# A two-layer attention trunk on one core: a second projection by seven block products, its root in a diagonal matrix, and three smaller moves

## The chip, the core and the metric

The kernel runs on one core of a Trainium2 chip. The metric is the device time of one execution in microseconds. A core has TensorE (PE, with its weight loads PEld), VectorE (DVE), ScalarE (ACT), GpSimd (POOL) and SyncE (SP), and 16 DMA engines that move data between HBM and the on-chip memories SBUF and PSUM. [...]

## The reference

256 tokens of width 2048 go through two layers and a final norm. Cut to what matters:

```python
h = x
h = h + gla_mixer(rms_norm(h, gla_norm), ...)        # layer 0
h = h + retention_mixer(rms_norm(h, ret_norm), ...)  # layer 1
return rms_norm(h, final_norm)

def gla_mixer(h, w_in, w_a1, w_a2, b_a, head_g, w_out):
    q, k, v, gate = split(h @ w_in)                  # 1024, 1024, 4096, 4096 columns
    log_a = log_sigmoid((h @ w_a1) @ w_a2 + b_a) / 16   # low-rank gate, rank 16
    o = chunked gated linear attention(q, k, v, log_a)  # 4 heads of 256 keys and 1024 values
    o = o * rsqrt(mean(o * o, -1) + EPS)             # per head and token
    return (o * head_g * silu(gate)) @ w_out         # 4096 -> 2048
```

The retention layer has the same outline: 8 heads of 256 keys and 512 values, rotary q and k, a group norm and a gated output projection of 4096 to 2048.

## The kernel before

**Precision.** Weights come from HBM as fp32 tiles `raw` of 2 x 128 x 512 elements (512 KB). `emit_split` turns each into a high part `hi` (ACT, L298) and a low part `lo` (DVE, L299). Activations lie in SBUF as such pairs too, transposed: `xhl` for layer inputs and `ogt` for gated head outputs, each with 16 tiles (kt) of 128 contraction rows x 256 tokens. Every product of a weight tile and an activation tile is three matmuls (high x high, high x low, low x high): L341 to L343 in plain groups, L412 to L414 in block products. Plain fp32 products appear only in small places, such as the scores' `pair_mm` (L763) and the transposes (L707) by an identity matrix.

**Plain and seven-product columns.** A plain group of 512 columns (`group_x`) runs eight weight tiles, 12 matmuls each. `out_pair` and `values_and_gates` treat two column groups together: the contraction's first half (kt 0 to 7) is a 2 x 2 block product, tokens by columns, made of seven block products (P1, P2, P3, P5, P6, P7, P8, of two weight tiles and 12 matmuls each) instead of eight; the second half runs directly (`direct`: v4 to v7 and g4 to g7, 12 matmuls for one weight tile). P1, P2 and P8 use the activations as they are; P3, P5, P6 and P7 use sums and differences of token blocks, which `make_sums` prepares (DVE and ACT) and splits. On the weights' side the sums are made in the raw tiles, by accumulating DMAs of POOL's queue and by DVE (L293). The order of the weight tiles is written out in strings such as `UNIT = "P1 v4 z P3 v5 P5 v6 P6 P2 v7 P7 g4 g5 P8 g6 g7"`; `_plan` turns the whole kernel's order into a list of loads and buffers beforehand. `next_weights` keeps the splits `LOOK = 3` tiles ahead, in four buffers for `hi` and `lo` each.

**Side work.** Latency-bound pieces are generators in `side` (GLA) or `tasks` (retention); `advance` runs one step of the first at set places between weight tiles, `drain_side` all that is left. A scheduler then sets each engine's order from this program order, the data's readiness in its own model and marks such as `high_priority`; `keep` holds instructions in program order, and `first` puts instructions at the front.

**Order.** Layer 0 runs heads 0 and 1, then the first half of its output projection (`out_half` "ga"), heads 2 and 3, and the second half ("gb"). Layer 1 does the same with four heads each, and ends with `out_last` and `out_tail`. `JOINT` says which value/gate groups and which column pairs go by seven products: in "gb" columns 0 and 1 are plain, 2 and 3 a pair.

**Head outputs.** `gla_head` makes each head's outputs in two groups of 512 columns: `o_part` (attention output, sums of squares `sso`), then `og_part`: the root `hr` of the head's mean square, `o * hr * silu(gate)` (L895), and `transpose_out` into `ogt`, four transposes for each half, with the head's scale applied on the way out (ACT L500, DVE L501). For head 3 this happens while "gb" is already running on kt 0 to 7.

**Low-rank gate.** `first_group` runs beside the first q/k group. At j = 0 it splits `w_a1` into `wa1` (ACT L613, DVE L614), and from j = 1 on it issues two `zps` products (L640) for each step, for the x tiles that `make_xhl` (L546, L549) has made.

**The tail.** The last 512 output columns are done last (`out_tail`), one half of the tokens t after the other. `tail_banks` puts the residual into PSUM first: one bank for t = 0, two banks of 256 columns for t = 1, whose matmuls are all 256 wide. Then come squares of both halves (ACT L1163), the product with the final norm's weights (DVE L1164), the root (`rsqrt_col`, L1125 to L1130), and the scaling of all columns (L1178, L1180) with their DMAs out.

Of the kernel before, what the change touches and what calls it, by code (L numbers as in the profile page):

```python
# [64 lines left out]
def _plan():  # L65
# [41 lines left out]
    def out_cols_of(name, half, cut, joint):  # L107
        for c in (0, 2):
            cols = [(name, half, c + n) for n in range(2)]
            if joint[c // 2]:  # L110
                pair(cols[1], cols[0])
# [45 lines left out]
UNIT = "P1 v4 z P3 v5 P5 v6 P6 P2 v7 P7 g4 g5 P8 g6 g7"  # L157
MIXED = "q0 q1 P1 q2 q3 q4 z P5 q5 P6 q6 q7 P2 P3 v4 v5 v6 P7 v7 g4 g5 P8 g6 g7"
WHOLE = " ".join(f"q{j}" for j in range(NSUB)) + " " + UNIT


def ret_order(h):
# [8 lines left out]
    ("ao", 0): (True, True),  # L171
    ("ao", 1): (False, True),
    ("ro", 0): (False, True),
# [5 lines left out]
def kernel(  # L179
# [260 lines left out]

    def make_sums(lhs, name, where):
        s = cur["s"] = [None] * 4
        room = where(name)
# [164 lines left out]
    def first_group(j):  # L608
        if j == 0:
            for kt in (2, 3):  # L610
                make_xhl(kt)
            first(
                nc.scalar.activation(wa1[:, :, 0:16], wa1_src, AF.Copy),  # L613
                nc.vector.tensor_tensor(  # L614
                    wa1[:, :, 32:48], wa1_src, wa1[:, :, 0:16].bitcast(F32), ALU.subtract
                ),
            )
        if j == 3:
# [4 lines left out]
        if j == 6:  # L623
# [7 lines left out]
            for hh in range(2):  # L631
# [5 lines left out]
                wa2.append(t)  # L637
        kts = range(2 * (j - 1), 2 * j) if j < NSUB - 1 else range(2 * (j - 1), NKT)
        for kt in kts if j else ():
            mm(zps, wa1[:, kt, :], xhl[:, kt, :, :], start=kt == 0, stop=kt == NKT - 1)  # L640
# [59 lines left out]

    def transpose_out(src, kt0, scale0, dst, name):
        for half in range(2):
            tp = mis_p.tile([P, 2, SEQ], F32, tag="mis", name=f"{name}_tp{half}")
            for jj in range(2):
                j = half * 2 + jj
                for t in range(2):
                    nc.tensor.transpose(  # L707
                        tp[:, jj, t * P : (t + 1) * P], src(t, j), ident
                    )
            kt = kt0 + half * 2  # L710
# [125 lines left out]
    def gla_head(h):  # L836
# [43 lines left out]
        def og_part(gj):  # L880
            g = 2 * h + gj
            if gj == 0:
# [9 lines left out]
            o, sg, hr = os_[gj], sgs[gj], hw["hr"]  # L892
            with tc.high_priority():
                for t in range(2):
                    nc.vector.scalar_tensor_tensor(  # L895
                        o[:, t, :], o[:, t, :], hr[:, t : t + 1], sg[:, t, :], ALU.mult, ALU.mult
                    )
            yield
# [4 lines left out]
                ogt,  # L903
                f"got{g}",
            )
# [72 lines left out]
    def tail_banks(t):  # L978
        w = GW // 2 if t else GW
        ps = acc(2, f"tail_ps{t}", (P, w), which=[2, 3]) if t else acc(1, f"tail_ps{t}", which=[1])  # L980
        for n, p in enumerate(ps):
            keep(nc.scalar.activation(p, cur["resid"][:, t, 3 * GW + n * w : 3 * GW + (n + 1) * w], AF.Copy))
        return ps

    def out_pair(c, first, name, final=False):
        lhs, s = ogt, cur["s"]
# [37 lines left out]
        product(A, plain(0, 0), stop=True)  # L1024
        advance()
        direct(lhs, (C, V1), 4)
        join(g, 0, A)
        advance()
        product(C, summed(0))
        advance()  # L1030
        direct(lhs, (C, V1), 5)
        drain_side()
        product(P5, summed(1), stop=True)
        direct(lhs, (C, V1), 6)
        for t in range(2):
            join(c, t, P5)
        product(A, summed(2), stop=True)
        product(B, plain(4, 0))
        join(c, 0, A, ALU.subtract)
        direct(lhs, (C, V1), 7, stop=True)  # L1040
        product(A, summed(3), stop=True)
# [25 lines left out]
        if onward:  # L1067
            for _ in late[0]:
                pass
            tasks.append(out_transposes(g))  # L1070
        begun.clear()
# [26 lines left out]
    def out_half(first, final, name, cut=0, hook=None, joint=(False, False)):  # L1098
        pend = {}
        for c in range(4):  # L1100
            if joint[c // 2]:
                if c % 2 == 0:
                    out_pair(c, first, name)
                continue
# [27 lines left out]
    def out_tail():  # L1132
# [5 lines left out]
        for t in range(2):  # L1138
# [4 lines left out]
            for j in range(HEAD, NSUB):  # L1143
                if t == 0:
                    kept.append(next_weights())
                hi, lo = kept[j - HEAD]
                if t == 0:
                    for q in range(SUB):
                        mm3(ps[0], ogt, j * SUB + q, t, hi, lo, q, HEAD * SUB)
                    continue  # L1150
                cols = [slice(0, half), slice(half, GW)]
                order = [(q, n) for q in range(SUB) for n in range(2)]
                if j == NSUB - 1:
                    order = [(q, n) for n in range(2) for q in range(SUB)]
                for q, n in order:
                    mm3(ps[n], ogt, j * SUB + q, t, hi[:, :, cols[n]], lo[:, :, cols[n]], q, HEAD * SUB)
            sq = st_p.tile([P, 2], F32, tag="sq", name=f"sq{t}")
            last = o_p.tile([P, 2, GW], F32, tag="o", name=f"last{t}")[:, 0, :]
            for n in range(2):
                at = slice(n * half, (n + 1) * half)  # L1160
                src = ps[n] if t else ps[0][:, at]
                junk = sg_p.tile([P, half], F32, tag="sg", name="sqj")
                nc.scalar.activation(junk, src, AF.Square, accum_out=sq[:, n : n + 1])  # L1163
                nc.vector.tensor_tensor(last[:, at], src, fns[3][:, at], ALU.mult)  # L1164
                if n == 0:
                    nc.vector.tensor_scalar(pre[:, 2:3], sq[:, 0:1], 1.0 / D, pre[:, 1:2], ALU.mult, ALU.add)
            rf = fin[:, 0, t : t + 1]
            rsqrt_col(rf, sq[:, 1:2], pre[:, 2:3], f"nf{t}")
            for piece, src, which in (
# [6 lines left out]
                src = cur["resid"][:, t, piece] if src is None else src  # L1176
                if which == "v":
                    nc.vector.tensor_scalar(src, src, rf, None, ALU.mult)  # L1178
# [281 lines left out]
    for h in range(2, 4):  # L1460
        gla_head(h)
    get_resid("gb_resid")
    slots = deque((2, 3, 0, 1))
    out_half(False, False, "gb", joint=JOINT["ao", 1])
# [123 lines left out]
```

## Time and profile before

| | |
|---|---|
| median of 3 runs | 1374.34 us (1373.69 to 1375.95) |
| profiled execution | 1373.26 us, span of the profile 1371.5 us |
| granted TensorE clock | 0.999 |
| PE busy | 1362.3 us, 99% |
| PEld, DVE, ACT, POOL busy | 1145.0, 1098.4, 847.0, 136.8 us |
| moved by DMA | 315.04 MB, mean 230 GB/s |

A row of a timeline has the start and duration in us, engine, line, operation, output<-inputs, shape and count, and in brackets the idle time of the engine before it with what ended it. A row of the groups has count, busy time, mean ns of one, and idle time before. A row of a stretch has, for each engine, busy us and instructions. L12 is line 12 of the kernel before.

### The profile page before, as it was taken

What the parts mean: (1) busy time and instruction counts of PE and PEld (TensorE: products, weight loads), DVE (VectorE), ACT (ScalarE), POOL (GpSimd) and SP (SyncE); (2) the same over time, 40 slices, a digit from 0 to 9 for tenths busy, and PEclk for the clock granted to TensorE, in tenths of its full rate; (3) what the DMA queues carried; (4) which work ended last, traced back from release to release, by engine and by line L of the source; (5) the groups of instructions that cost most, each with busy time, mean ns of one, the idle gap of its engine ahead of it and who ended that gap; (6) DMA issues with size and microseconds to landing.
All of it is one profiled execution on the core that took longest, in us unless ns stands there. A gap on an engine that the chain in (4) does not pass through costs nothing.

```text
span 1371.5 us, 18372 instructions
## 1 busy us (share of the span) xinstructions
PE 1362.3 (99%) x6564; PEld 1145.0 (83%) x6564; DVE 1098.4 (80%) x1520; ACT 847.0 (62%) x1119; POOL 136.8 (10%) x194
## 2 busy tenths in 40 slices
PE   9999999999999999999999999999999999999997
PEld 8888888888888888888888888888888888888886
DVE  6686795987878896769887988897867897889796
ACT  6576656656567756656666576655546665666565
POOL 1003020110021021001011010100101101010010
PEclk9999999999999999999999999999999999999999
DMA  9755566789658667868897878796798797979773
GB/s 358 259 175 168 169 208 184 156 247 318 200 153 262 204 204 183 319 169 232 267 331 197 260 202 249 207 316 218 172 367 219 240 261 197 259 198 317 241 176 124
DMA packets 84508, 315.04 MB, mean 230 GB/s; under 512 B 9776, under 2 KB 10800, under 8 KB 83136
## 3 DMA queue, kind: packets, MB, share of 16 engines
q1 hardware_dynamic: 67200, 241.63, 50.4%
q0 software_dynamic: 15920, 64.89, 23.9%
q10 hardware_dynamic: 1296, 7.35, 1.4%
q8 instruction: 51, 0.84, 0.2%
q14 instruction: 41, 0.34, 0.1%
HBM read 303.35 MB, written 10.49 MB: 229 GB/s over the span
## 4 chain that ended last, share of the span: by engine, by line
PE 99%; DMA 1%; DVE 0%; ACT 0%; DVEq 0%; issue 0%; ACTq 0%
PE rqk_ps L384 8%; PE re_ps L412 8%; PE re_ps L413 8%; PE re_ps L414 8%; PE rqk_ps L385 4%; PE gqk_ps L384 4%; PE gg_ps L342 3%; PE gv_ps L343 3%; PE gv_ps L341 3%; PE gv_ps L342 3%; PE gg_ps L341 3%; PE gg_ps L343 3%; PE ge_ps L412 2%; PE ge_ps L413 2%; PE ge_ps L414 2%; PE gae_ps L413 2%
## 5 line engine op out<-in xcount | busy, mean ns | idle before, releaser
L299 DVE TENSOR_TENSOR lo<-raw,hi 128x1024 fp32r<-128x1024 f32 (+1 forms) x568 | 687.4, 1221 | 215.5 <-ACT hi L298 205.5
L298 ACT ACTIVATE hi<-raw 128x1024 fp32r<-128x1024 f32 (+1 forms) x568 | 595.9, 1055 | 394.3 <-DMA raw<-in_w_all 50.8
L384 PE MATMUL rqk_ps<-xhl,hi 128*128 128x512 f32 x480 | 162.9, 397 | 0.0
L413 PE MATMUL re_ps<-lo,xhl 128*128 128x512 f32 x352 | 137.5, 391 | 0.0
L414 PE MATMUL re_ps<-hi,xhl 128*128 128x512 f32 x352 | 137.3, 390 | 0.0
L310 POOL DMA_DIRECT2D raw<-in_w_all x90 | 78.0, 868 | 556.1 <-DVE lo L299 222.1
L412 PE MATMUL re_ps<-hi,xhl 128*128 128x512 f32 x352 | 132.6, 391 | 0.0
L385 PE MATMUL rqk_ps<-xhl,lo 128*128 128x256 f32 x480 | 122.5, 281 | 0.0
L384 PEld LDWEIGHTS rqk_ps<-xhl,hi 128*128 128x128 f32 x480 | 89.7, 188 | 17.8
L385 PEld LDWEIGHTS rqk_ps<-xhl,lo 128*128 128x128 f32 x480 | 87.6, 189 | 3.4
L414 PEld LDWEIGHTS re_ps<-hi,xhl 128*128 128x128 f32 x352 | 66.1, 188 | 13.6
L413 PEld LDWEIGHTS re_ps<-lo,xhl 128*128 128x128 f32 x352 | 66.2, 188 | 13.2
L412 PEld LDWEIGHTS re_ps<-hi,xhl 128*128 128x128 f32 x352 | 66.0, 188 | 13.2
L384 PE MATMUL gqk_ps<-xhl,hi 128*128 128x512 f32 x216 | 76.6, 399 | 0.0
L342 PE MATMUL gg_ps<-lo,xhl 128*128 128x512 f32 x192 | 75.5, 393 | 0.0
L342 PE MATMUL gv_ps<-lo,xhl 128*128 128x512 f32 x192 | 75.3, 392 | 0.0
L341 PE MATMUL gv_ps<-hi,xhl 128*128 128x512 f32 x192 | 75.2, 393 | 0.0
L343 PE MATMUL gv_ps<-hi,xhl 128*128 128x512 f32 x192 | 75.1, 391 | 0.0
L343 PE MATMUL gg_ps<-hi,xhl 128*128 128x512 f32 x192 | 75.0, 391 | 0.0
L341 PE MATMUL gg_ps<-hi,xhl 128*128 128x512 f32 x192 | 74.9, 392 | 0.0
L829 POOL TENSOR_TENSOR s<-s,m 128x64 f32<-128x64 f32 x56 | 36.1, 676 | 232.5 <-DVE m L820 223.2
L385 PE MATMUL gqk_ps<-xhl,lo 128*128 128x256 f32 x216 | 59.1, 281 | 0.0
(434 smaller groups left out, 2659.8 us busy)
## 6 DMA issues: line engine op xcount, KB each, us to landing
raw<-in_w_all SPq DMA_DIRECT2D x449, 512.0 KB, 4.9
raw<-in_w_all POOLq DMA_DIRECT2D x90, 512.0 KB, 6.8
resid<-in_x_n SPq DMA_DIRECT2D x2, 1024.0 KB, 10.8
gg<-in_gn_g POOLq DMA_DIRECT2D x8, 256.0 KB, 4.2
resid_x<-resid ACTq DMA_DIRECT2D x1, 2048.0 KB, 7.9
gb<-in_gn_b POOLq DMA_DIRECT2D x8, 256.0 KB, 6.0
gb_resid<-resid_x POOLq DMA_DIRECT2D x1, 2048.0 KB, 11.3
resid_g<-gb_resid ACTq DMA_DIRECT2D x1, 2048.0 KB, 10.5
```

What stands on the lines that cost most here:

```text
L298: a = nc.scalar.activation(hi[:, sl], src[:, sl], AF.Copy)
L299: b = nc.vector.tensor_tensor(lo[:, sl], src[:, sl], hi[:, sl].bitcast(F32), ALU.subtract)
L310: nc.gpsimd.dma_start(raws[n], block(key), accum_op=ALU.add)
L341: pin(mm(ps, xh, hi[:, q, :], start=kt == 0, stop=False, **onto))
L342: pin(mm(ps, xh, lo[:, q, :], start=False, stop=False, **onto))
L343: pin(mm(ps, xl, hi[:, q, :], start=False, stop=kt == end - 1, **onto))
L384: mm(ps[c], wh, rhs[:, kt, :, :], start=kt == 0, stop=False)
L385: mm(ps[c][:, 0, :], wl, rhs[:, kt, 0, :], start=False, stop=False)
L412: pin(mm(ps, xh, hi[:, q, :], start=start, stop=False, **again))
L413: pin(mm(ps, xh, lo[:, q, :], start=False, stop=False, **again))
L414: pin(mm(ps, xl, hi[:, q, :], start=False, stop=stop, **again))
L829: nc.gpsimd.tensor_tensor(dst, dst, side_of(m[:, li, :], z), ALU.add)
```

## The change

It has five parts. (1) Columns 0 and 1 of "gb" become a pair by seven products, in a new order `LATE` that has P1, P2, P3 first and the tiles kt 8 to 15 (v4 to v7) late. Its sums ("osum2") are made in five steps within the last value/gate stage of head 3 (group 7) and serve columns 2 and 3 too. (2) For head 3, `o` is multiplied by the gate without the root; the root goes into a diagonal matrix that takes the identity's place, so the transposes become fp32 matmuls. (3) `wa1` is split at j = 2, and the `zps` products run two steps later, eight of the 16 at the end. (4) In the tail t = 1 has one bank of 512 columns, and only its last weight tile runs in halves. (5) The last 256 columns are multiplied by norm weight and root in one instruction, behind the root.

```diff
+LATE = "P1 P2 z P3 v4 P5 v5 P6 v6 v7 P7 g4 g5 P8 g6 g7"
 JOINT = {
-    ("ao", 1): (False, True),
+    ("ao", 1): (True, True),
...
 def first_group(j):
         if j == 0:
             for kt in (2, 3):
                 make_xhl(kt)
-            first(
-                nc.scalar.activation(wa1[:, :, 0:16], wa1_src, AF.Copy),
-                nc.vector.tensor_tensor(
-                    wa1[:, :, 32:48], wa1_src, wa1[:, :, 0:16].bitcast(F32), ALU.subtract
-                ),
-            )
+        if j == 2:
+            nc.scalar.activation(wa1[:, :, 0:16], wa1_src, AF.Copy)
+            nc.vector.tensor_tensor(wa1[:, :, 32:48], wa1_src, wa1[:, :, 0:16].bitcast(F32), ALU.subtract)
...
-        kts = range(2 * (j - 1), 2 * j) if j < NSUB - 1 else range(2 * (j - 1), NKT)
-        for kt in kts if j else ():
+        kts = range(2 * (j - 3), 2 * (j - 2)) if j < NSUB - 1 else range(2 * (j - 3), NKT)
+        for kt in kts if j > 2 else ():
             mm(zps, wa1[:, kt, :], xhl[:, kt, :, :], start=kt == 0, stop=kt == NKT - 1)
...
 def transpose_out(src, kt0, scale0, dst, name, diag=None):
-                    nc.tensor.transpose(
-                        tp[:, jj, t * P : (t + 1) * P], src(t, j), ident
-                    )
+                    to = tp[:, jj, t * P : (t + 1) * P]
+                    if diag is None:
+                        nc.tensor.transpose(to, src(t, j), ident)
+                    else:
+                        mm(to, src(t, j), diag[:, t, :], start=True, stop=True)
...
 def og_part(gj):
+            scaled = h == GLA_H - 1
+            if scaled and gj == 0:
+                hw["diag"] = sc_p.tile([P, 3, P], F32, tag="s32", name=f"hd{h}", bufs=1)
+            if scaled:
+                with tc.high_priority():
+                    for t in range(2):
+                        nc.vector.tensor_tensor(o[:, t, :], o[:, t, :], sg[:, t, :], ALU.mult)
...
                     rsqrt(hr, m, 2, f"hr{h}")
+                    if scaled:
+                        for t in range(2):
+                            nc.vector.tensor_scalar(hw["diag"][:, t, :], ident, hr[:, t : t + 1], None, ALU.mult)
...
+        making = make_sums(ogt, "osum2", sums_in_v, "next_s") if h == 3 else None
         def joint_turn(tok):
+            if making and tok in ("P3", "P5", "P6", "v7", "g6"):
+                next(making)
...
 def tail_banks(t):
-        w = GW // 2 if t else GW
-        ps = acc(2, f"tail_ps{t}", (P, w), which=[2, 3]) if t else acc(1, f"tail_ps{t}", which=[1])
+        ps = acc(1, f"tail_ps{t}", which=[1 + t])[0]
...
 def out_pair(c, first, name, final=False, late_direct=False):
         product(A, plain(0, 0), stop=True)
+        if late_direct:
+            product(B, plain(4, 0))
+            join(g, 0, A)
+            product(C, summed(0))
+            while len(side) > 1:
+                advance()
+            advance()
+            direct(lhs, (C, V1), 4)
+            advance()
+            product(P5, summed(1), stop=True)
+            advance()
+            direct(lhs, (C, V1), 5)
+            for t in range(2):
+                join(c, t, P5)
+            drain_side()
+            product(A, summed(2), stop=True)
+            direct(lhs, (C, V1), 6)
+            join(c, 0, A, ALU.subtract)
+            direct(lhs, (C, V1), 7, stop=True)
+        else:
...
 def out_tail():
-                if t == 0:
+                if t == 0 or j < NSUB - 1:
                     for q in range(SUB):
-                        mm3(ps[0], ogt, j * SUB + q, t, hi, lo, q, HEAD * SUB)
+                        mm3(ps, ogt, j * SUB + q, t, hi, lo, q, HEAD * SUB)
                     continue
...
+                for at in (slice(0, half), slice(half, GW)):
+                    for q in range(SUB):
+                        mm3(ps[:, at], ogt, j * SUB + q, t, hi[:, :, at], lo[:, :, at], q, HEAD * SUB)
...
                 nc.scalar.activation(junk, src, AF.Square, accum_out=sq[:, n : n + 1])
-                nc.vector.tensor_tensor(last[:, at], src, fns[3][:, at], ALU.mult)
                 if n == 0:
+                    nc.vector.tensor_tensor(last[:, at], src, fns[3][:, at], ALU.mult)
...
+                if src is last:
+                    at = slice(half, GW)
+                    nc.vector.tensor_scalar(last[:, 0:half], last[:, 0:half], rf, None, ALU.mult)
+                    nc.vector.scalar_tensor_tensor(last[:, at], ps[:, at], rf, fns[3][:, at], ALU.mult, ALU.mult)
```

More of the change, by code (lines that the diff above doesn't have):

```diff
@@ L110, in out_cols_of @@
             if joint[c // 2]:
-                pair(cols[1], cols[0])
+                pair(cols[1], cols[0], order=LATE if cols[0] == ("ao", 1, 0) else None)
                 continue
@@ L889, in og_part @@
                     rsqrt(hr, m, 2, f"hr{h}")
+                    if scaled:
+                        for t in range(2):
+                            nc.vector.tensor_scalar(hw["diag"][:, t, :], ident, hr[:, t : t + 1], None, ALU.mult)
                 hw["hr"] = hr
                 yield
[L892 to L897, printed above, removed]
+            hr = hw["hr"]
+            if not scaled:
+                with tc.high_priority():
+                    for t in range(2):
+                        nc.vector.scalar_tensor_tensor(
+                            o[:, t, :], o[:, t, :], hr[:, t : t + 1], sg[:, t, :], ALU.mult, ALU.mult
+                        )
             yield
@@ L1024, in out_pair @@
         product(A, plain(0, 0), stop=True)
[L1025 to L1040, printed above, removed]
+        if late_direct:
[10 more added lines that the diff above has]
+            direct(lhs, (C, V1), 5)
+            for t in range(2):
+                join(c, t, P5)
[5 more added lines that the diff above has]
+        else:
+            advance()
+            direct(lhs, (C, V1), 4)
+            join(g, 0, A)
+            advance()
+            product(C, summed(0))
+            advance()
+            direct(lhs, (C, V1), 5)
+            drain_side()
+            product(P5, summed(1), stop=True)
+            direct(lhs, (C, V1), 6)
+            for t in range(2):
+                join(c, t, P5)
+            product(A, summed(2), stop=True)
+            product(B, plain(4, 0))
+            join(c, 0, A, ALU.subtract)
+            direct(lhs, (C, V1), 7, stop=True)
         product(A, summed(3), stop=True)
@@ L1102, in out_half @@
                 if c % 2 == 0:
-                    out_pair(c, first, name)
+                    out_pair(c, first, name, late_direct=c == 0 and name == "gb")
                 continue
@@ L1462 @@
     get_resid("gb_resid")
+    cur["s"] = cur["next_s"]
     slots = deque((2, 3, 0, 1))
```

25 lines of the change are left out of this document (10 added, 15 removed).

## The prediction

> **What bounds the kernel now.** I read the page first, its engine shares, then the list of who waited for whom on PE, then PE's timeline for the pace of one matmul, and last the timelines of the three places that the change touches.
>
> ```profile
> PE 1362.3 (99%) x6564; PEld 1145.0 (83%) x6564; DVE 1098.4 (80%) x1520; ACT 847.0 (62%) x1119; POOL 136.8 (10%) x194
> ```
>
> ```profile
> PE warm_ps L521 <- POOL lnone L523: 1.0, 1, 1.0
> PE zps L640 <- DVE wa L614: 0.4, 1, 0.4
> ```
>
> PE is busy 1362.3 us, 99% of the span, and the list of its waits has two lines for the whole run: 1.0 us at the warm-up and 0.4 us at the first low-rank product. Everything between is issued back to back. So what counts is the number of PE instructions times their pace, the wait at the head, the chain after the last matmul, and any wait that the change creates. Work on the other engines costs nothing as long as PE does not see it.
>
> A matmul is listed with 0.39 us, but they overlap; the pace is the distance of the starts.
>
> ```profile
> 565.06 0.39 PE L341 MATMUL gb_ps<-hi,ogt 128*128 128x512 f32 x1
> ...
> 569.14 0.39 PE L341 MATMUL gb_ps<-hi,ogt 128*128 128x512 f32 x1
> ```
>
> These two are 18 matmuls apart: 4.08 / 18 = 0.227 us each. A matmul removed is worth 0.227, not 0.39.
>
> **The seven products (gain 2.7).** The first two column blocks of the second GLA output projection go from plain to the form that the last two have.
>
> ```profile
> L342 PE MATMUL gb_ps<-lo,ogt 128*128 128x512 f32 x64 | 24.9, 391 | 0.0
> L413 PE MATMUL gbe_ps<-lo,ogt 128*128 128x512 f32 x44 | 17.2, 392 | 0.0
> L412 PE MATMUL gbe_ps<-hi,osum 128*128 128x512 f32 x12 | 4.8, 398 | 0.0
> L412 PE MATMUL gbe_p<-hi,osum 128*128 128x512 f32 x4 | 1.6, 390 | 0.0
> ```
>
> Each row is one of three lines with equal counts. Plain: 3 x 64 = 192. By products: 3 x (44 + 12 + 4) = 180. The saving is 12 matmuls, since only half of the contraction is in the 2x2 block form: 12 x 0.227 = -2.72 us.
>
> **The root in a diagonal matrix (cost 1.8).** The 16 transposes of head 3 become products with a diagonal fp32 matrix of the same shape. A transpose is one PE instruction; an fp32 product is two.
>
> ```profile
> L707 PE MATMUL got_tp<-ident,go 128*128 128x128 f32 x64 | 9.4, 272 | 0.0
> L763 PE MATMUL lv<-w 128*128 128x128 f32 x112 | 15.7, 274 | 0.0
> ```
>
> The first is 8 groups of columns x 8 transposes = 64, one each. L763 is called for 7 levels x 2 halves x 4 heads = 56 products and has 112 instructions.
>
> ```profile
> 196.21 1.05 PE L763 MATMUL lv<-w 128*128 128x128 f32 x8
> 197.10 0.61 PE L763 MATMUL lv<-w_x 128*128 128x128 f32 x4
> ...
> 366.64 1.05 PE L763 MATMUL lv<-w 128*128 128x128 f32 x8
> 367.45 0.48 PE L341 MATMUL gv_ps<-hi,xhl 128*128 128x512 f32 x1
> ...
> 579.14 0.60 PE L707 MATMUL got_tp<-ident,go 128*128 128x128 f32 x4
> 579.50 0.71 PE L343 MATMUL gb_ps<-hi,ogt 128*128 128x512 f32 x2
> ```
>
> Four transposes take 579.50 - 579.14 = 0.36 us, eight instructions of four fp32 products 367.45 - 366.64 = 0.81. The difference is 0.45 for a group of four, and there are four groups: +1.8 us. Bounds: 1.4 if the extra 16 go at the transposes' 0.09, and 2.1 by the slowest eight (197.10 - 196.21 = 0.89). [...]
>
> What the diagonal buys is latency: o times gate no longer waits for the root. PE did not wait there, so by itself that is worth nothing.
>
> **The low-rank gate later (gain 0.2, between -0.5 and +0.9).**
>
> ```profile
> 10.29 1.23 DVE L299 TENSOR_TENSOR lo<-raw,hi 128x1024 fp32r<-128x1024 f32 x1 [0.37 <-ACT hi L298]
> 11.05 0.63 PE L374 MATMUL gqk_ps<-xhl,lo 128*128 128x256 f32 x4
> 11.12 0.42 ACT L613 ACTIVATE wa<-wa_src 128x256 fp32r<-128x256 f32 x1 [0.86 <-DMA wa_src<-in_w_a]
> ...
> 11.97 1.29 DVE L549 SCALAR_TENSOR_TENSOR xhl<-xt,head,xhl 128x256 fp32r<-128x256 f32 x3
> 12.05 1.12 PE L640 MATMUL zps<-xhl,wa 128*48 128x512 f32 x4 [0.37 <-DVE wa L614]
> ```
>
> PE's four 256-column matmuls from 11.05 are issued by 11.5, and it restarts at 12.05 when the gate weights are split: 0.5 us lost. Without them ACT takes the next x tile earlier, but VectorE is on L299 until 11.52 and its L549 (1.29 for three) then needs over 0.4, so the first matmul of the next x tile starts near 12.0 as well, unless VectorE takes the two in the other order. The four zps products that filled 12.05 to 13.0 (4 x 0.23 = 0.9) come later, so PE stands 0.9 us closer to the x tiles that are still arriving. So the wait is half moved, not removed: -0.5 if it goes, +0.9 if all of that cover was needed, and I take -0.2, since the row shows weights and x just in time rather than late.
>
> **The tail (cost 0.7).** For the second 128 tokens three of four steps become 512 wide: 36 matmuls of 256 columns become 18. At the ends: first 256-wide at 1357.75, last at 1363.38 of 48, so 5.63 / 47 = 0.120 each; 36 x 0.120 - 18 x 0.227 = 0.24 us less PE.
>
> ```profile
> 1357.52 0.39 PE L343 MATMUL tail_ps<-xhl,ogt 128*128 128x512 f32 x1
> 1357.75 0.28 PE L341 MATMUL tail_ps<-xhl,ogt 128*128 128x256 f32 x1
> ...
> 1358.01 0.38 ACT L1163 ACTIVATE sqj<-tail_ps 128x256 f32<-128x256 f32 x1 [0.15 <-PE tail_ps L343]
> ...
> 1358.97 0.38 ACT L1163 ACTIVATE sqj<-tail_ps 128x256 f32<-128x256 f32 x1 [0.49 <-DVE last L1164]
> ...
> 1360.44 0.21 DVE L1130 TENSOR_SCALAR fin<-nf_nw 128x1 f32<-128x1 f32 x1
> ...
> 1362.98 0.38 ACT L1163 ACTIVATE sqj<-tail_ps 128x256 f32<-128x256 f32 x1 [1.17 <-PE tail_ps L343]
> ...
> 1363.38 0.28 PE L343 MATMUL tail_ps<-xhl,ogt 128*128 128x256 f32 x1
> ...
> 1363.70 0.38 ACT L1163 ACTIVATE sqj<-tail_ps 128x256 f32<-128x256 f32 x1 [0.24 <-PE tail_ps L343]
> ...
> 1364.20 0.42 DVE L1164 TENSOR_TENSOR last<-tail_ps,fn 128x256 f32<-128x256 f32 x1 [0.17 <-ACT sqj L1163]
> ...
> 1365.36 0.21 DVE L1130 TENSOR_SCALAR fin<-nf_nw 128x1 f32<-128x1 f32 x1
> ...
> 1366.27 0.48 DVE L1178 TENSOR_SCALAR last<-last,fin 128x512 f32<-128x512 f32 x1
> ```
>
> Two banks let the second half of the tokens square its first columns at 1362.98, under the last matmuls. The first half of the tokens already uses one bank, and there the second square (1358.97) waits 0.49 us for VectorE's read of the other half of the bank. With one bank for the second tokens too, both squares come after the last matmul, one behind the other. The root is ready (end of L1130) 1365.57 - 1363.70 = 1.87 us after the first square behind PE today; in the one-bank pattern it is 1360.65 - 1358.01 = 2.64, of which about 0.05 goes because L1164's second half is no longer in VectorE's queue: +0.72. Behind the root the last columns take a 256-wide scaling (about 0.25, half of the 512-wide 0.48) and a 256-wide read from PSUM (0.42, as L1164) instead of one of 0.48: +0.19. Tail: -0.24 + 0.72 + 0.19 = +0.67. Were the squares not held by the bank, only the second L1164 (0.42, in VectorE's queue ahead of the root) would go, and the tail would be -0.24 - 0.42 + 0.19 = -0.5 at best.
>
> **The work that is moved in front of the projection (cost 0.6, between 0 and 4.5).** The sums over the chunks, made today during the second plain column, move into head 3's last value-and-gate stage, and the projection begins with three products in a row.
>
> ```profile
> 556.00:566.00 10.00, 10.00 (x46) 8.29 (x45) 8.46 (x18) 7.41 (x13) 0.00 (x0) 1.00 1.01 419
> 566.00:576.00 10.00, 10.00 (x50) 8.33 (x49) 8.66 (x13) 6.29 (x9) 0.00 (x0) 1.00 0.71 228
> ...
> 644.00:655.00 11.00, 11.00 (x54) 9.06 (x53) 11.00 (x15) 6.64 (x9) 0.00 (x0) 1.00 0.84 277
> ```
>
> ```profile
> L299 DVE TENSOR_TENSOR lo<-raw,hi 128x1024 fp32r<-128x1024 f32 x564 | 684.8, 1224 | 214.4 <-ACT hi L298 204.4 <-DMA raw<-in_w_all 3.8
> ...
> L501 DVE SCALAR_TENSOR_TENSOR ogt<-got_tp,smalls,ogt 128x256 fp32r<-128x256 f32 x32 | 14.8, 479 | 3.5 <-ACT ogt L500 3.4
> ...
> L464 DVE TENSOR_TENSOR osum<-osum_f,osum 128x512 fp32r<-128x512 f32 x8 | 5.2, 686 | 1.2 <-ACT osum L463 1.2
> ```
>
> (Columns of the first: PE, PEld, DVE, ACT, POOL busy.) A product takes a new weight tile every 6 matmuls, 1.36 us; the plain form every 12, 2.72. In the 8.2 us of P1, P2, P3 VectorE splits six tiles instead of three (+3 x 1.22 = 3.7), and has the last two splits of the sums (1.4) and the two halves of the diagonal (about 0.5) beside the gating and the copies behind the transposes that it has now. 556 to 576 holds 8.46 + 8.66 = 17.1 of 20 us; 22.7 would be wanted. Splits run three tiles ahead, which is 4 us of products, so most of the excess of 2.7 is borrowed, and 644 to 655 shows VectorE at 11.00 of 11.00 with PE losing nothing. The second danger is the first transposed tile: today the first reader of what the transposes give is the fifth step of plain matmuls, afterwards the transposes stand directly in front of their reader v4, and their copies (ACT, then L501 with 0.48; ACT's taken as equal) come to about 1 us with the hand-overs, 1.5 with two in a row. Half of the next column group's products are issued in between and hide most of it. Lower bound 0, upper 2.7 + 1.5 and a hand-over, 4.5; I take +0.6, nearest to the row at 11.00. The pair of columns has 20 half-megabyte transfers (14 loads, 6 accumulated through POOL's queue) instead of 16 loads. An accumulated one takes 6.8 us to land:
>
> ```profile
> raw<-in_w_all POOLq DMA_DIRECT2D x90, 512.0 KB, 6.8
> ```
>
> The first pair is used again after P2, P3 and v4, 3 x 2.72 = 8.2 us, which hides it by 1.4; I cost it at nothing, and at most what is short of that.
>
> **Sum.** -2.72 + 1.8 - 0.2 + 0.67 + 0.6 = +0.15 us on the profiled execution's 1373.26, that is 1373.4. The median of the runs is 1.08 us above that execution, so I predict 1374.5. Measured against no change this kernel can tell about 0.2%, 2.7 us: the forecast is no change.
>
> **Rivals.** *PE starves at the start of the second projection* (0.20): VectorE's excess and the copies behind the transposes land on PE. For it: the 22.7 us wanted in 20, and three products in a row. Against: the saturated stretch at 644. Price: 3.5 to 4.5 in place of 0.6, so +3.0 to +4.0 and 1377.4 to 1378.4, slower. It decides if PE waits over 3.2 us in all between head 3's last gate matmul and v7.
>
> [...]
>
> *The diagonal is nearly free and nothing is serialized* (0.08): if the diagonal products go at a transpose's price (0), the tail gains 0.5, the head its 0.5 and nothing starves, the sum is -2.72 - 0.5 - 0.5 = -3.7: 1370.6, faster. Against it: two instructions per fp32 product, and the 0.49 us wait for a bank.
>
> **Numbers.** The forecast has 0.68; its lower end is the lower bounds together, -2.72 + 1.4 - 0.5 - 0.5 = -2.3, and its upper end the 2.7 of no change. Slower: 0.20 + 0.04 = 0.24; faster 0.08. The range 1372.0 to 1377.9 goes from that lower end to the middle of the first rival; it leaves out the third rival and the upper half of the first.
>
> **What would show it.** PE in the after profile: 12 fewer 512-wide matmuls in the second projection, 32 instructions at the diagonal transposes at about 0.1 us distance, 18 wide and 12 narrow in the last tokens; the zps wait gone from the list or replaced by one on xhl; first square of the second tokens after the last matmul, root about 2.6 us behind it; and no wait of PE above 1 us near v4. A sum of PE waits over 3 us there makes the first rival true; one instruction per diagonal product, the third.

## The result and the profile after

The changed kernel takes 1377.65 us (median of 13 runs, 1375.89 to 1379.82), the kernel before in the same job 1374.21 (13 runs, 1372.95 to 1375.95): ratio 1.0027, interval 1.0020 to 1.0034. It is slower by 3.4 us. The profiled execution took 1375.89 us with a span of 1374.1; it is the shortest of its 13, so 1.8 us of the median are not in it. The profile before lies 0.95 us under its own median, so some 0.8 us of the difference are in neither; a profile of a longer execution below bears on them.

PE's row of the page after, and the list of who waited for whom on PE:

```profile
PE 1361.3 (99%) x6550; PEld 1142.4 (83%) x6550; DVE 1109.0 (81%) x1535; ACT 853.4 (62%) x1125; POOL 142.3 (10%) x200
```

```profile
PE gbe_ps L413 <- ACT hi L299: 1.8, 1, 1.8
PE warm_ps L522 <- POOL lnone L524: 1.0, 1, 1.0
PE gbe_p L414 <- DVE lo L300: 0.7, 1, 0.7
PE gqk_ps L373 <- DVE xhl L550: 0.4, 1, 0.4
PE gqk_ps L373 <- ACT hi L299: 0.3, 1, 0.3
```

PE is busy 1.0 us less than before. The zps wait of the head is gone; two on x and on a weight tile (0.4 and 0.3) stand in its place. And two waits are in the second projection: 0.7 within P5 (`gbe_p`) and 1.8 in front of P6. This is the stretch (timeline after, rows of the root, of the splits and of PE):

```profile
562.50 0.15 DVE L895 TENSOR_TENSOR hm<-sso 128x2 f32<-128x2 f32 x1
...
572.77 2.36 DVE L300 TENSOR_TENSOR lo<-raw,hi 128x1024 fp32r<-128x1024 f32 x2
572.96 0.39 PE L413 MATMUL gbe_p<-hi,osum 128*128 128x512 f32 x1
574.04 0.50 PE L414 MATMUL gbe_p<-lo,osum 128*128 128x512 f32 x1 [0.70 <-DVE lo L300]
...
575.04 0.16 DVE L498 SCALAR_TENSOR_TENSOR hr<-hr_nw 128x2 f32<-128x2 f32 x1
575.11 1.22 DVE L300 TENSOR_TENSOR lo<-raw,hi 128x1024 fp32r<-128x1024 f32 x1
576.25 2.35 DVE L294 TENSOR_TENSOR raw<-raw,raw 128x1024 f32<-128x1024 f32 x2
576.48 0.40 PE L415 MATMUL gbe_p<-hi,osum 128*128 128x512 f32 x1
577.58 2.19 ACT L299 ACTIVATE hi<-raw 128x1024 fp32r<-128x1024 f32 x2 [2.89 <-DVE raw L294]
578.52 0.48 DVE L900 TENSOR_SCALAR hd<-ident,hr 128x128 f32<-128x128 f32 x2
578.69 0.50 PE L413 MATMUL gbe_ps<-hi,osum 128*128 128x512 f32 x1 [1.81 <-ACT hi L299]
579.03 1.95 PE L709 MATMUL got_tp<-hd,go 128*128 128x128 f32 x16
...
580.73 0.48 PE L414 MATMUL gbe_ps<-lo,osum 128*128 128x512 f32 x1
```

From start to start PE loses 574.04 - 572.96 - 0.23 = 0.85 and 578.69 - 576.48 - 0.23 = 1.98, together 2.83. VectorE's rows point to the reason: the same ten microseconds in the kernel before and after (columns: PE, PEld, DVE, ACT, POOL busy with counts):

```profile
572.00:582.00 10.00, 10.00 (x53) 8.37 (x52) 6.33 (x9) 5.89 (x10) 0.00 (x0) 1.00 0.70 209
```

```profile
572.00:582.00 10.00, 7.49 (x40) 5.86 (x40) 10.00 (x15) 5.38 (x7) 3.07 (x4) 1.00 0.68 181
```

VectorE's busy time went from 6.33 to 10.00 us of the ten, and the root of head 3 is taken in thirteen small steps that stand between splits of 1.2 us and other large instructions in this queue: from 562.50 to 575.20, 12.7 us. In the kernel before, the first and the last step are

```profile
561.79 0.16 DVE L887 TENSOR_TENSOR hm<-sso 128x2 f32<-128x2 f32 x1
...
566.02 0.16 DVE L497 SCALAR_TENSOR_TENSOR hr<-hr_nw 128x2 f32<-128x2 f32 x1
```

that is 561.79 to 566.18, 4.4 us. After the root, in the changed kernel, the diagonal stands behind one more split and two sums of raw tiles, until 578.52. So the transposes come at 579.03, and v4, which the order has in front of P5, is not there to fill PE while VectorE catches up.

The rest agrees with what the prediction said would show. Groups of the products (each row is one of three lines with equal counts) and of the diagonal, and the timeline of the last tokens, all after:

```profile
L414 PE MATMUL gbe_ps<-lo,ogt 128*128 128x512 f32 x88 | 34.6, 393 | 0.0
...
L414 PE MATMUL gbe_ps<-lo,osum 128*128 128x512 f32 x24 | 9.5, 396 | 0.0
...
L414 PE MATMUL gbe_p<-lo,osum 128*128 128x512 f32 x8 | 3.2, 406 | 0.7 <-DVE lo L300 0.7
```

```profile
L709 PE MATMUL got_tp<-hd,go x32: 270/275/275, 579.0 to 590.0; 128*128 128x128 f32 x32
```

```profile
1365.21 0.28 PE L344 MATMUL tail_ps<-xhl,ogt 128*128 128x256 f32 x1
1365.53 0.38 ACT L1195 ACTIVATE sqj<-tail_ps 128x256 f32<-128x256 f32 x1 [1.73 <-PE tail_ps L344]
...
1366.50 0.38 ACT L1195 ACTIVATE sqj<-tail_ps 128x256 f32<-128x256 f32 x1 [0.49 <-DVE last L1197]
...
1367.88 0.21 DVE L1165 TENSOR_SCALAR fin<-nf_nw 128x1 f32<-128x1 f32 x1
```

### The profile page after: what moved, and what is told of

The parts are those of the page before. It is cut to its first block, busy times and chain, and to the rows that moved or that the text cites. A ratio compares the mean times of both kernels' runs of the same rounds, so it can differ in the third digit from the quotient of the medians.

```text
span 1374.1 us, 18390 instructions
## 1 busy us (share of the span) xinstructions
PE 1361.3 (99%) x6550; PEld 1142.4 (83%) x6550; DVE 1109.0 (81%) x1535; ACT 853.4 (62%) x1125; POOL 142.3 (10%) x200
## 4 chain that ended last, share of the span: by engine, by line
PE 98%; DVE 1%; DMA 0%; issue 0%; ACT 0%; SPq 0%; DVEq 0%; ACTq 0%
PE rqk_ps L385 8%; PE re_ps L413 8%; PE re_ps L415 8%; PE re_ps L414 8%; PE rqk_ps L386 4%; PE gqk_ps L385 4%; PE gg_ps L343 3%; PE gv_ps L343 3%; PE gv_ps L342 3%; PE gv_ps L344 3%; PE gg_ps L342 3%; PE gg_ps L344 3%; PE ge_ps L414 2%; PE ge_ps L413 2%; PE ge_ps L415 2%; PE gae_ps L413 2%
## 5 line engine op out<-in xcount | busy, mean ns | idle before, releaser
L311 POOL DMA_DIRECT2D raw<-in_w_all x96 | 83.3, 869 | 554.3 <-DVE lo L300 328.9
```

Of the source, the lines that this page charges most:

```text
L311: nc.gpsimd.dma_start(raws[n], block(key), accum_op=ALU.add)
```

## The experiments

Two theories were tested for the waits. ROOT: the root's steps, spread over VectorE's queue, bring the diagonal late, and PE has no v4 in front of P5 and P6. SUPPLY: the weight tiles of P5 and P6 come late whatever else there is, since each is a sum made by an accumulating DMA or by VectorE.

**1. Plain columns, all else as changed.**

```diff
-    ("ao", 1): (True, True),
+    ("ao", 1): (False, True),
...
-        making = make_sums(ogt, "osum2", sums_in_v, "next_s") if h == 3 else None
+        making = make_sums(ogt, "osum2", sums_in_v, "next_s") if h == 3 and JOINT["ao", 1][0] else None
...
-    cur["s"] = cur["next_s"]
```

> The changed kernel with columns 0 and 1 of the second GLA projection plain again (part 1 undone; diagonal, head and tail as changed). Both theories of the two PE waits in the pair's first products (0.85 and 1.98 us) expect them gone, and 12 more matmuls: -2.8 + 2.7, about the changed kernel's time, and 2.7 to 3 us over the kernel before, which is then the price of the diagonal (2.0) and the tail (0.9) alone. If it comes within 1 us of the kernel before, the diagonal and the tail cost next to nothing and the pair costs it all.

Measured: 1376.03 us (1375.2 to 1376.66), ratio 1.0014 [1.0005, 1.0024], and no wait of PE in the projection. The time is 1.9 us over the kernel before, less than the 2.7 to 3 expected. From the projection's first matmul to the retention layer's first value group (`rs`, a mark that is used again below) it is 565.98 to 729.95, before 565.06 to 727.29: 1.74 us longer, the price of the diagonal with no wait around it.

**2. The root's Newton steps on GpSimd.**

```diff
+        if pool:
+            h, g = s[:, 2, :], s[:, 3, :]
+            nc.gpsimd.tensor_scalar(h, m, -0.5, None, ALU.mult)
+            for it in range(3):
+                nc.gpsimd.tensor_tensor(a, b, b, ALU.mult)
+                nc.gpsimd.tensor_tensor(a, a, h, ALU.mult)
+                nc.gpsimd.tensor_scalar(a, a, 1.5, None, ALU.add)
+                nc.gpsimd.tensor_tensor(y if it == 2 else b, a, b, ALU.mult)
+            return
...
-                    rsqrt(hr, m, 2, f"hr{h}")
+                    rsqrt(hr, m, 2, f"hr{h}", pool=h == GLA_H - 1)
```

> The changed kernel with the three Newton steps of head 3's root on GpSimd instead of VectorE. Theory ROOT: the waits come because the root's 13 small dependent operations are spread over 12.7 us of VectorE's queue (4.4 before), so the diagonal is ready at 579 instead of 568 and v4, which was to fill the time in front of P5 and P6, is not there. It expects the diagonal by 570, v4 within P5, the two waits (2.8 us) gone to under 0.5, and 2.5 us less than the changed kernel, about 1375. Theory SUPPLY: P5's and P6's weight tiles come late in any case (the accumulating DMA landed 10.9 us after its issue), so the same waits appear in front of P5 and P6 behind v4, and it gains under 1 us.

Measured: 1374.95 us (1374.1 to 1375.85), ratio 1.0007 [0.9998, 1.0016]. Its timeline:

```profile
566.90 1.14 POOL L501 TENSOR_SCALAR hr_nw<-hr_nw 128x2 f32<-128x2 f32 x1
...
570.43 0.20 POOL L502 TENSOR_TENSOR hr<-hr_nw 128x2 f32<-128x2 f32 x1
570.65 0.48 DVE L909 TENSOR_SCALAR hd<-ident,hr 128x128 f32<-128x128 f32 x2 [0.94 <-POOL hr L502]
571.90 1.95 PE L718 MATMUL got_tp<-hd,go 128*128 128x128 f32 x16
...
576.98 2.35 DVE L294 TENSOR_TENSOR raw<-raw,raw 128x1024 f32<-128x1024 f32 x2
...
579.82 0.39 PE L413 MATMUL gbe_ps<-hi,osum 128*128 128x512 f32 x1
581.00 1.13 PE L718 MATMUL got_tp<-hd,go 128*128 128x128 f32 x8 [0.79 <-DVE ogt L511]
```

The root is ready 4.6 us sooner, the transposes come at 571.90 instead of 579.03, and both waits are gone. One of 0.95 from start to start is new, for the copies behind the transposes. The sums of raw tiles from which P6's weights are made (L294) are not ready sooner: they end at 579.33, in the changed kernel at 578.60, and the two projections start within 0.1 us of each other. Yet P6 starts at 579.82 without a wait, because the transposes and most of v4 run in front of it. From the projection's start to the mark it is +0.37 over the kernel before; the changed kernel (564.80 to 729.44) is at +2.41.

**3. Transposes in place of the diagonal.**

```diff
-            scaled = h == GLA_H - 1
+            scaled = False
```

> The changed kernel with head 3 by plain transposes again, and o times root times gate in one operation behind the root (part 2 undone). 16 fewer PE instructions and no diagonal: -1.96 us by the spacing in the changed kernel's trace (0.106 for each of 32 against 0.09 for 16). Theory ROOT: the two operations of the diagonal also leave VectorE's queue, the transposes can stand in front of P5, and most of the 2.8 us of waits goes too: -3 to -4.5 in all, 1373 to 1374.5. Theory SUPPLY: -2 only, waits as before, 1375.6.

Measured: 1375.25 us (1373.88 to 1377.44), ratio 1.0007 [0.9998, 1.0017]. The profiled execution is its longest, and the waits moved rather than went:

```profile
PE gbe_ps L413 <- ACT hi L299: 0.9, 1, 0.9
PE got_tp L707 <- DVE go L907: 0.8, 1, 0.8
```

The diagonal is gone, and PE now waits for the gate product (L907), which needs the root; a wait of 0.9 in front of P6 (1.10 from start to start) stays, although the transposes and most of v4 now run ahead of it. The ratio is 0.0020 under the changed kernel's, some 2.7 us, between the 2 that SUPPLY expected and the 3 to 4.5 of ROOT, so this run does not decide between them. The same thirteen steps took 7.8 us here: how far they are spread depends on the order in which VectorE's instructions were set.

**4. The head and the tail alone, on the kernel before.** Parts 3, 4 and 5 as in the change's diff.

> The kernel before with only parts 3, 4 and 5: the later low-rank gate, the wide tail and the last columns scaled at once. By the two traces the head should be level (first score matmul at 92.3 against 92.4 us) and the tail 0.8 us longer (span end 8.9 us behind the last matmul against 8.1, less 0.24 of PE): +0.6 to +0.9 us. If the tail is free, no difference; if the head's new waits count (0.44 and 0.51 against 0.52), +1.2.

Measured: 1373.74 us (1372.96 to 1375.11), ratio 0.9997 [0.9988, 1.0006]: nothing of the loss is here that could be measured. The interval ends at +0.8 us, so the 0.5 us that the traces show for the tail can be in it.

**5. The changed kernel again, on another chip.**

> The changed kernel once more, for a second profile: the first one was the shortest of its 13 executions (1375.89 of a median of 1377.65). Theory ROOT plus a late weight tile: the waits in front of P5 and P6 are there again and longer by what the execution is longer (3 to 5 us in all), since what P5 waits for is an accumulating DMA among many others. If the extra lies anywhere else (a wait at another place, a longer tail), the two waits are not the whole of the loss.

Measured: 1377.41 us (1375.96 to 1379.16, 6 runs), ratio 1.0028 [1.0016, 1.0040]. The profiled execution took 1378.58, 2.7 more than the first. Its two waits are 0.85 and 2.08 from start to start (0.7 and 1.9 in the list of its waits), hardly longer, against what was expected; what is new is PE's pace behind them. Stretches of this execution, and the third one of the first (columns: PE busy, granted clock, DMA share, GB/s):

```profile
578.00:579.00 1.00, 0.00 (x0) 1.00 0.94 143
579.00:580.00 1.00, 0.54 (x2) 0.88 0.84 344
580.00:583.00 3.00, 3.00 (x16) 0.50 0.93 138
583.00:584.00 1.00, 1.00 (x7) 0.91 1.01 193
```

```profile
580.00:583.00 3.00, 3.00 (x19) 1.00 1.00 167
```

For about 3.4 us behind the wait the granted clock is one half (3 us at 0.50, and parts of the stretches at 0.88 and 0.91), which costs 1.7 us if PE does half as much in that time: an estimate from the clock of these stretches. How much of the median this explains is worked out below.

**6. Seven products without the diagonal, root on GpSimd, old head and tail.** Experiments 2 and 3 together, `first_group`, `tail_banks` and `out_tail` as before.

> The seven products alone, with what they were found to lack: the pair of columns as changed, Newton steps of head 3's root on GpSimd, plain transposes, head and tail as before. By the terms measured so far: -2.72 for 12 matmuls, no diagonal, no tail, and a wait of up to 1 us in front of the second transposes: 1.7 to 2.7 us under the kernel before, 1371.5 to 1372.5. If the seven products bring waits whatever is done about the root (theory SUPPLY), it is level with the kernel before.

Measured: 1375.45 us (1374.9 to 1377.96), ratio 1.0012 [1.0003, 1.0022]: missed by some 4 us. Its waits and a stretch:

```profile
PE got_tp L719 <- DVE go L919: 1.8, 2, 1.5
```

```profile
573.00:576.00 3.00, 3.00 (x11) 0.50 0.05 20
```

Without the diagonal the gate product hangs on the root again (four of 0.7 us behind it), and the transposes stand early in PE's order: some 2.2 us are lost in front of and between the first eight, and here too the clock is at one half behind it. So the diagonal does buy something: it takes the gate product out of the chain.

**7. One PSUM bank for the second tokens, widths as before** (one execution).

```diff
-        ps = acc(2, f"tail_ps{t}", (P, w), which=[2, 3]) if t else acc(1, f"tail_ps{t}", which=[1])
+        ps = acc(1, f"tail_ps{t}", which=[1 + t])
+        if t:
+            ps = [ps[0][:, 0:w], ps[0][:, w:GW]]
```

> The kernel before with one thing changed: the second tokens' last columns in one PSUM bank instead of two, at the same 256-wide matmuls. If the bank serializes, the first square starts behind the last matmul instead of 0.4 us ahead of it, the second waits about 0.5 us for VectorE's read, and the root is ready 2.6 us behind the first square instead of 1.9 behind the second. If only instructions on the same bytes wait, the tail is as before.

Measured: 8.89 us from the last matmul to the end instead of 8.12, +0.77, with the same 0.49 in the bracket as in the changed kernel:

```profile
1368.20 0.38 ACT L1165 ACTIVATE sqj<-tail_ps 128x256 f32<-128x256 f32 x1 [0.49 <-DVE last L1166]
```

The execution as a whole took 1377.58, with waits at 316, 916 and 995 us that have nothing to do with the edit; only its end is read here.

**8. The last columns scaled at once, alone** (one execution). Part 5 of the change's diff on the kernel before.

> The kernel before with only part 5: the last 256 columns by norm weight and root in one instruction behind the root. The second L1164 leaves the chain in front of the root (-0.05 to -0.3), and the end of the last scaling is 0.2 later against the root. Span behind the last matmul: 8.0 to 8.3 us against 8.1.

Measured: 7.91 us from the last matmul to the end, -0.21; 1373.17 in all. The root is ready 0.28 sooner, and the end lies 0.07 further behind it. Experiments 9 and 11, with the same tail, have 7.94 and 7.96.

**9. Root on GpSimd with the diagonal, old head, old tail with part 5 alone.**

> Seven products and the diagonal kept, the Newton steps of head 3's root on GpSimd, head as in the kernel before, tail as in the kernel before with only the last columns scaled at once. ROOT (the root's small dependent steps, spread over VectorE's queue, leave TensorE with nothing to fill in front of P5 and P6): the terms measured so far are -2.72 (seven products), +1.96 (diagonal), +0.95 (the one wait that was left with the root on GpSimd) and -0.21 (last columns at once), in all 0.0 against the kernel before, ratio 0.9995 to 1.0005, no wait of TensorE over 1 us in front of P6. SUPPLY (the tiles of P5 and P6 come late whatever else there is): 2 us of waits are there again, +2. On the granted clock: a wait of 0.95 us left no stretch at half clock in the run with the root on GpSimd, so no run here below 0.998.

Measured: 1374.04 us (1372.94 to 1374.93, 11 runs) beside 1373.77, ratio 1.0003 [0.9994, 1.0011]; one wait of 0.95, and no run with a granted clock under 0.998. ROOT had expected a ratio of 0.9995 to 1.0005, no such wait over 1 us and no such run, SUPPLY +2 us. The same stretch of this kernel:

```profile
572.00:582.00 10.00, 9.21 (x53) 7.75 (x52) 10.00 (x13) 5.89 (x9) 1.82 (x2) 1.00 0.47 119
```

VectorE is as full as in the changed kernel, 10.00, and PE does 9.21 of 10 instead of 7.49: not the load by itself but what stands behind it decides. No run kept the thirteen steps together in VectorE's queue, so what another order alone would do stays open.

**10. Half of the residual loaded later, on the changed kernel.**

```diff
+    def rest_resid(after):
+        n = D // 2
+        nc.scalar.activation(cur["resid"][:, 0, D - 1 : D], after[:, 0:1], AF.Copy)
+        nc.gpsimd.dma_start(cur["resid"][:, :, n:D], cur["resid_at"][:, :, n:D])
...
+            rest_resid(P5)
...
-    get_resid("gb_resid")
+    get_resid("gb_resid", True)
```

Only column groups 0 and 1 are loaded at the start; groups 2 and 3 follow once P5 is there.

> The changed kernel with one thing else: of the 2 MB residual that is loaded at the start of the second projection only the first two column groups (1 MB) are loaded there, the other 1 MB behind P5 (one 128x1... one-element ScalarE copy of P5's bank into the part not yet loaded holds that load back until then). The root stays in VectorE's queue. SUPPLY: with 1 MB less in the stretch in which all DMA engines are busy (546 to 566 us) the accumulated weight tiles come about 2.5 us sooner (1 MB at the 410 GB/s of that stretch), so the wait of 0.85 in front of P5 goes, the one of 1.98 in front of P6 falls below 1, and the median falls by 2 to 3.5 us against the changed kernel, to a ratio of 1.000 to 1.001 against the kernel before. ROOT: v4 is as late as before, since the root's steps still stand between the splits; the wait in front of P6 stays at 1.5 or more, the ratio at 1.002 or above. In between: only the 0.85 goes, ratio 1.002. Clock: if the wait of 2 us stays, some 4 in 10 runs at 0.997 or less.

Measured: 1378.01 us (1377.41 to 1379.21, 6 runs), ratio 1.0034 [1.0022, 1.0047]. Timeline:

```profile
572.70 1.06 ACT L299 ACTIVATE hi<-raw 128x1024 fp32r<-128x1024 f32 x1 [0.30 <-PE gbe_ps L415]
...
574.94 0.50 PE L414 MATMUL gbe_p<-lo,osum 128*128 128x512 f32 x1 [0.70 <-DVE lo L300]
...
578.48 2.20 ACT L299 ACTIVATE hi<-raw 128x1024 fp32r<-128x1024 f32 x2 [3.37 <-DVE raw L294]
579.59 0.50 PE L413 MATMUL gbe_ps<-hi,osum 128*128 128x512 f32 x1 [1.81 <-ACT hi L299]
```

ScalarE no longer waits for a DMA in this place (it did, 1.19 us, in the changed kernel), and PE's two waits are the same to the last digit, 0.70 and 1.81. So SUPPLY falls as far as a late DMA is meant. From start to mark: +2.41, as in the changed kernel.

**11. Both, 9 and 10.**

> The kernel with the root on GpSimd, the old head, the old tail and the last columns at once, with the residual loaded in two halves as well. ROOT: the two waits in front of P5 and P6 are gone already, so the half load brings nothing: within 0.3 us of the kernel with the whole load, ratio 0.9995 to 1.0005 against the kernel before. SUPPLY: the wait of 0.95 that was left is worth having too; another 0.5 to 1 us less, ratio 0.999 to 0.9995, faster than both kernels.

Measured: 1373.78 us (1373.09 to 1377.03, 11 runs), ratio 1.0003 [0.9994, 1.0012]: the half load brings nothing here either. Experiments 9 and 11 are the best versions with the seven products, and both are level with the kernel before.

**12. A longer root in the kernel before.**

```diff
-        for it in range(3):
+        for it in range(steps):
...
-                    rsqrt(hr, m, 2, f"hr{h}")
+                    rsqrt(hr, m, 2, f"hr{h}", 7 if h == GLA_H - 1 else 3)
```

> The kernel before with seven Newton steps for head 3's root in place of three, twelve small VectorE instructions more in the same chain, nothing else; the outputs stay the same. ROOT: the chain takes some 8 us in place of 4.4 (13 instructions in 4.4 us, so 25 in 8.4), the transposes of head 3 stand behind 48 matmuls in TensorE's queue instead of 29 (48 x 0.227 = 10.9 us behind the projection's start), and their copies and first readers come right behind them: TensorE waits 1 to 3 us in this place, though not one product, sum or diagonal is changed, and the time goes up by that much, ratio 1.001 to 1.002. If nothing is waited for, the plain columns cover a late root and only the seven products' order made it matter; ratio 0.9995 to 1.0005. Clock: if a wait of 1.8 us or more is there, some 4 in 10 runs have a granted clock of 0.997 or less, each 1.7 us longer than the others, as in the changed kernel and in no run of the kernel before; with waits below 1 us none.

Measured: 1374.81 us (1374.11 to 1375.81, 11 runs) beside 1373.62, ratio 1.0008 [0.9999, 1.0017].

```profile
571.64 0.16 DVE L497 SCALAR_TENSOR_TENSOR hr<-hr_nw 128x2 f32<-128x2 f32 x1
...
578.07 0.50 PE L341 MATMUL gb_ps<-hi,ogt 128*128 128x512 f32 x1 [0.64 <-ACT ogt L500]
```

The root is ready at 571.80 instead of 566.18, and PE loses 0.97 from start to start in this row; from start to mark it is +1.76. So a late root alone costs time, with no product, sum or diagonal changed, and the plain columns cover most of it. The interval of the runs doesn't separate the loss from nothing, but the trace shows it. No run had a granted clock under 0.998.

## Why the prediction was wrong, step by step

The prediction's sum was +0.15 us and its forecast no change; the kernel became 3.4 us slower, clear of the spread. That 1377.65 lies inside the stated range, which went up to 1377.9, is no merit of the sum: the range was stretched to the middle of the first rival. Nor is 0.2% the least that can be told here; 13 runs of each kernel gave an interval of 0.07% to either side.

- *Seven products, -2.72.* The count is right: 3 x (88 + 24 + 8) = 360 matmuls for four column groups, against 192 + 180 = 372. In time: +2.41 from start to mark, less waits of 2.83 and a diagonal of 1.74, leaves -2.2; experiment 9 gives 0.36 - 0.95 - 1.74 = -2.3. So some 0.4 less than worked out; where that lies stays open.
- *Diagonal, +1.8.* Right: +1.74 in experiment 1; 32 instructions on PE, the first 16 in 580.73 - 579.03 = 1.70, 0.106 each. The 0.04 in the prediction's chance of slower (0.20 + 0.04) stands for diagonal products at four times a transpose, which no run shows: two instructions of 0.106 against one of 0.09 are 2.4 times.
- *Low-rank gate, -0.2.* Nothing that can be told: the projection starts at 564.80 instead of 565.06 in this execution, but over all profiles it starts at 564.80 to 565.98 with the new head and at 564.64 to 565.67 with the old one. A wait on x and one on weights took the place of the one on zps.
- *Tail, +0.67.* Nearly right: +0.77 behind the last matmul (8.89 for 8.12) and -0.24 on PE, +0.53. The root is ready 1368.09 - 1365.53 = 2.56 behind the first square, predicted 2.6. The bank's price stands (+0.77 in experiment 7, 0.72 predicted). Behind the root it is 1374.1 - 1368.09 = 6.01 in place of 1371.5 - 1365.57 = 5.93: +0.08, where +0.19 was put for the last scaling. The -0.21 of experiment 8 doesn't add to this: its gain is the second L1164 leaving the queue in front of the root, 0.28 with two banks and only some 0.1 with one.
- *Work moved in front of the projection, +0.6.* This is the step that failed. It measured +2.83 in the waits, and the estimate adds 1.7 in the executions where the clock halved. The prediction had VectorE's excess (22.7 us wanted in 20) and took 0.6 because in 644 to 655 VectorE was full and PE lost nothing. That row was the wrong neighbour: no chain of small dependent steps is in VectorE's queue there, only instructions of 0.68 us and more. Here the root was in it, and its thirteen steps, 4.4 us before, took 12.7. The prediction said of the diagonal's gain in latency that "by itself that is worth nothing"; it had looked at where PE waited, not at what would delay the root. With the root on GpSimd the same step measured 0.95 (experiments 2 and 9), near the 0.6.
- *The first rival* had the place, the direction and the size (1377.4 to 1378.4), and of its two reasons VectorE's excess, but not the root: the copies behind the transposes, its other reason, are no releaser of the two waits. Its condition, over 3.2 us of waits, wasn't quite reached (2.83 and 2.93 in the two profiles). That the time fits nevertheless is in part luck: the clock and the smaller gain of the products made up the rest.

The sum as measured, on the profiled executions: -0.26 at the head, +2.41 to the mark, -0.08 until the tail, -0.24 and +0.77 in it, 2.6 in all, the difference of the spans (1374.1 - 1371.5). The medians differ by 0.8 more, and the clock is the likely reason: of 25 runs of the changed kernel (experiments 5 and 10 included) 11 have a mean granted clock of 0.997 or less, where half a clock for 3.4 us is 0.0012 of the span. Without experiment 10 the medians are 1378.4 for those and 1376.6 for the others, and the latter is 2.4 above the kernel before, about what the spans differ by. In the kernel before and in experiments 1 to 4, 9, 11 and 12, where no wait in this place is over 1.1 us, no run is under 0.998 of those whose clock is on record. What decides whether a wait of 2 us is followed by half a clock stays open: the profile of experiment 5 had it and the first one not, behind nearly the same waits.

## What to carry to other kernels

When a change makes an engine full for ten microseconds, look for a chain of small dependent steps in that engine's queue: here nine of the twelve steps behind the first came after at least one instruction of 0.68 us or more, and the chain stretched from 4.4 to 12.7 us although nothing was added to it. Moving the chain to GpSimd, which was 10% busy, gave back 2.0 us, nearly all that the seven products gain, though one of its small instructions took 0.20 to 1.14 us there (experiment 2) and 0.15 to 0.17 on VectorE. A stretch where a full engine cost nothing is only a neighbour for another one if the same kind of work hangs on it.

## What the runs showed of the hardware

Behind some 2 us lost on TensorE the granted clock was one half for about 3.4 us in two profiles: 0.50 from 580 to 583 us in experiment 5, with 0.88 and 0.91 in the microseconds beside it, and 0.50 from 573 to 576 in experiment 6, with 0.99 and 0.80 beside it. In experiment 6 the starts of four matmuls of 128x512 lie 0.43 us apart there (574.47, 574.90, 575.32, 575.75), in place of 0.227. The clock was 1.00 behind a wait of 1.98 in the first profile of the changed kernel. What sets the length, no run shows.

GpSimd instructions of 128 x 2 elements took 0.20 to 0.23 us, but 0.57 and 0.50 us when a gate product (L898) on VectorE had started before them, and 1.14 and 1.06 us when a split had. Timeline of experiment 2:

```profile
566.62 0.20 POOL L500 TENSOR_TENSOR hr_nw<-hr_nw 128x2 f32<-128x2 f32 x1
566.75 1.23 DVE L300 TENSOR_TENSOR lo<-raw,hi 128x1024 fp32r<-128x1024 f32 x1 [0.26 <-ACT hi L299]
566.90 1.14 POOL L501 TENSOR_SCALAR hr_nw<-hr_nw 128x2 f32<-128x2 f32 x1
```

The split ends at 567.98, GpSimd's instruction at 568.04: it lasted as long as what was left of the split. The other such split runs from 568.49 to 569.71, and the GpSimd instruction that started at 568.71 took 1.06 us and ended at 569.77. Why they end together, no run shows.
